# Newton's products of three normalizations kept in a PSUM bank, and y h y of one column as one operation

## The chip, the cores and the metric

The kernel runs on one core of a Trainium2 chip. The metric is the time of one execution on the device in microseconds (us); for the kernel before it is the median of three runs.

## What is computed

Two layers of a decoder trunk over 512 tokens of width 1024 in float32. Each layer is a half-step SwiGLU feed-forward (FFN a), a token mixer with three groups of heads (differential attention, dilated attention, RWKV-7), and a second half-step feed-forward (FFN b). A layer norm over the 1024 columns follows each of the three, and the RWKV-7 part normalizes its keys per head:

```python
def layer_norm(x, g, b):
    mu = jnp.mean(xf, -1, keepdims=True)
    var = jnp.mean(jnp.square(xf - mu), -1, keepdims=True)
    return (xf - mu) * lax.rsqrt(var + LN_EPS) * g + b
for l in range(DEPTH):
    x = layer_norm(ALPHA * x + 0.5 * swiglu(x, ffn_a...), ln_g[l, 0], ln_b[l, 0])
    ...                                    # input projection x @ w_in, three mixers
    kk = kk / jnp.maximum(jnp.sqrt(jnp.sum(jnp.square(kk), -1, keepdims=True)), 1e-12)
    ...
    x = layer_norm(ALPHA * x + mix @ w_out, ln_g[l, 1], ln_b[l, 1])
    x = layer_norm(ALPHA * x + 0.5 * swiglu(x, ffn_b...), ln_g[l, 2], ln_b[l, 2])
```

## The kernel before

**Tiling.** The 512 tokens are four tiles of 128 (t = 0 to 3). Every product runs as three float32r products of a high part and a low part (`mm3`, L85 to L87). A weight is split by ACT (`hi`, L79) and DVE (`lo`, L80) in the feed-forwards, and by ACT (`wh`) and POOL (`wl`, a subtraction of two SBUF tiles of 128x512) in the mixer.

**The reciprocal root.** `rsqrt_ops` (L89) starts from h = -v/2 (L94) and a first y by integer arithmetic (L97). Three Newton steps follow, of three DVE operations each: t = y y (L100), t = t h (L102), y = (t + 1.5) y (L104). All tiles are in SBUF, of n columns: n = 1 in the feed-forwards (one token tile), n = 2 in the norm behind the mixer (two token tiles at once), n = 8 in the keys, n = 4 and 8 in two other places (`rwkv_out`, `norms`).

**Feed-forward.** `project` (L145) makes the down projection. For each of the last token tiles `close` adds the accumulator, a PSUM bank, to x (L162), and takes statistics (L163); `norm_ops` (L129) then runs `bn_aggr` (L132), the Newton steps, and four operations on x of 128x512: x - mean times g (L139) and times the root plus b (L143). Tiles 0 and 1 come in the first half, their banks have the tag "r"; tiles 2 and 3 come last (tag "p1"), so that their norms stand between one stage and the next. A normalized tile is transposed on PE into PSUM banks (tag "m"), copied by ACT (`xhi`) and DVE (`xlo`). Here the framework's own scheduler orders the instructions.

**Mixer.** Streams (`keys`, `decays`, `columns`, `out`, `head` and others, in the order of `RANK`) are merged by `Board.merge`: it keeps an estimated time for every engine and tile, and counts free banks of each tag (`when`); the order that it emits is the order on each engine. A stream that needs a tag whose banks are all taken is held until another stream calls `drop`. In the trace all these operations have the line L504. At its start, columns for tokens 0 to 255 run on PE from tiles 0 and 1, and tiles 2 and 3 are transposed as soon as their norms of FFN a are done. `keys(j)` sums squares on PE into an "r" bank, copies them out (`ss`, a maximum with 1e-24), drops the bank, and runs the Newton steps with n = 8; PE then transposes the root. `out(half)` is the output projection of two tiles and their norm with n = 2; `head` begins FFN b on PE, with banks "p0" and "p1".

**Banks.** There are eight PSUM banks: two each of "p0", "p1", "m" and "r".

Of the kernel before, what the change touches and what calls it, by code (L numbers as in the profile page):

```python
# [8 lines left out]
FT = mybir.dt.float32  # L9
# [3 lines left out]
OP = mybir.AluOpType  # L13
# [4 lines left out]
NT = S // 128  # L18
# [9 lines left out]
class Trunk:  # L28
# [57 lines left out]
        mm(out, lh, rl, start=False, stop=False)  # L86
        mm(out, ll, rh, start=False, stop=last)  # L87

    def rsqrt_ops(self, pool, v, n, scale, eps, steps, vec):  # L89

        h = pool.tile([128, n], FT, name="rs_h", tag=f"rs_h{n}", bufs=2)
        y = pool.tile([128, n], FT, name="rs_y", tag=f"rs_y{n}", bufs=2)
        t = pool.tile([128, n], FT, name="rs_t", tag=f"rs_t{n}", bufs=2)
        vec.tensor_scalar(h, v, -0.5 * scale, -0.5 * eps, op0=OP.mult, op1=OP.add)  # L94
        yield y
        magic = 1597463007.0 - 2.0 ** 22 - 2.0 ** 30
        vec.tensor_scalar(y.bitcast(I32), h.bitcast(I32), -0.5, magic, op0=OP.mult, op1=OP.add)  # L97
        yield y
        for _ in range(steps):
            vec.tensor_tensor(t, y, y, op=OP.mult)  # L100
            yield y
            vec.tensor_tensor(t, t, h, op=OP.mult)  # L102
            yield y
            vec.scalar_tensor_tensor(y, t, 1.5, y, op0=OP.add, op1=OP.mult)  # L104
            yield y
# [20 lines left out]
    def stats(self, t):  # L126
        return self.const.tile([128, 2, 6], FT, name=f"st{t}", tag=f"st{t}", bufs=1)

    def norm_ops(self, ts, st, g, b, eps, vec):  # L129
        mv = self.const.tile([128, len(ts), 2], FT, name="mv", tag=f"mv{len(ts)}", bufs=2)  # L130
        for i, t in enumerate(ts):
            vec.bn_aggr(mv[:, i], st[t])  # L132
        for r in self.rsqrt_ops(self.const, mv[:, :, 1], len(ts), 1.0, eps, 3, vec):
            yield "."
        for i, t in enumerate(ts):
            x = self.x[t]
            for h in range(2):
                c = slice(h * 512, (h + 1) * 512)
                vec.scalar_tensor_tensor(x[:, c], x[:, c], mv[:, i, 0:1], g[:, 0, c], op0=OP.subtract, op1=OP.mult)  # L139
                yield "."  # L140
            for h in range(2):
                c = slice(h * 512, (h + 1) * 512)
                vec.scalar_tensor_tensor(x[:, c], x[:, c], r[:, i:i + 1], b[:, 0, c], op0=OP.mult, op1=OP.add)  # L143

    def project(self, h, w, alpha, eps, g, b, late):  # L145


        nc = self.nc
        nk = len(h)
        st = [self.stats(t) for t in range(NT)]  # L150

        def load(j, c):
            return self.weight(w[j * 256:(j + 1) * 256, c * 512:(c + 1) * 512].rearrange("(k p) c -> p k c", p=128), 2, 512)

        def step(acc, t, k, w2):
            hi, lo = h[k]
            s = slice(t * 128, (t + 1) * 128)
            self.mm3(acc, hi[:, s], lo[:, s], w2[0][:, k % 2, :], w2[1][:, k % 2, :], k == 0, k == nk - 1)

        def close(acc, t, c):  # L160
            xs = self.x[t][:, c * 512:(c + 1) * 512]
            nc.vector.scalar_tensor_tensor(xs, xs, alpha, acc, op0=OP.mult, op1=OP.add)  # L162
            nc.vector.bn_stats(st[t][:, c, :], xs)  # L163

        acc = [self.acc(("p0", "p1")[t // 2]) for t in range(NT)]
        for j in range(nk // 2):
            w2 = load(j, 0)
            for k in (2 * j, 2 * j + 1):
                for t in range(NT):
                    step(acc[t], t, k, w2)  # L170
        for t in range(NT):
            close(acc[t], t, 0)
        gt, bt = self.raw(self.row(g), 1, D), self.raw(self.row(b), 1, D)
        normed = []
        for half in range(2):
            ts = (2 * half, 2 * half + 1)
            acc = {t: self.acc("p1" if half else "r") for t in ts}
            tail = TAIL if half else 0
            for j in range(nk // 2 - tail):
                if half and j == TURN:  # L180
                    for t in normed:
                        self.to_channels(t)
                w2 = load(j, 1)
                for k in (2 * j, 2 * j + 1):
                    for t in ts:
                        step(acc[t], t, k, w2)
            rest = [(j, load(j, 1)) for j in range(nk // 2 - tail, nk // 2)]
            for t in ts:
                for j, w2 in rest:
                    for k in (2 * j, 2 * j + 1):  # L190
                        step(acc[t], t, k, w2)
                close(acc[t], t, 1)
                for _ in self.norm_ops((t,), st, gt, bt, eps, nc.vector):
                    pass
                if t not in late:
                    if half:
                        self.to_channels(t)
                    else:
                        normed.append(t)
# [163 lines left out]
class Board:  # L363
# [27 lines left out]
    def drop(self, *tiles):  # L391
        for t in tiles:
            r = self.ready[t.tensor.name]
            self.slots[r[3]].append(r[2])
            r[3] = "dropped"
# [118 lines left out]
class Mix:  # L514
# [360 lines left out]
    def keys(self, j):  # L875

        tr, P = self.tr, self.P
        vec, act, pe, sp = self.vec, self.act, self.pe, self.sp
        u, drop, ct = self.u, self.drop, self.ct
        v3 = lambda t, hf: t[:, hf * 256:(hf + 1) * 256].rearrange("p (c t) -> p c t", t=64)  # L880
        yield f"k{j}", "u"
        k = ct[f"k{j}"]
        q = u("kap")
        act.activation(q, k, AF.Square, scale=P("c_k_k", j))
        yield ".", "r"
        ps = self.acc("r", (128, NT, 2))
        for n in range(NT):
            pe.matmul(ps[:, n, :], q[:, n * 128:(n + 1) * 128], tr.pick, start=True, stop=True)
        yield "."
        ss = self.t("ss", (128, 8), bufs=2)  # L890
        vec.tensor_scalar(ss, ps.rearrange("p n e -> p (n e)"), 1e-24, None, op0=OP.max)
        drop(ps)
        for rs in tr.rsqrt_ops(self.pool, ss, 8, 1.0, 0.0, 3, vec):
            yield "."
        yield ".", "r"
        ps = self.acc("r", (2, S))
        for n in range(NT):
            pe.transpose(ps[:, n * 128:(n + 1) * 128], rs[:, 2 * n:2 * n + 2], tr.ident)
        act.copy(q[0:2], ps)
        drop(ps)  # L900
        yield ".", "r"
        ps = self.acc("r")
        pe.matmul(ps, self.c["sel"][0:2], q[0:2], start=True, stop=True)
        yield "."
        vec.scalar_tensor_tensor(q, k, P("c_k_k", j), ps, op0=OP.mult, op1=OP.mult)
        drop(ps)

        yield f"decays{j}", "u"
        a, dk, dr, db = self.key[j]
        t = u("kt")  # L910
        act.activation(t, a, AF.Identity, scale=P("c_k_a", j), bias=self.omka[:, j:j + 1])
        vec.tensor_tensor(a, a, q, op=OP.mult)
        yield "."
        vec.tensor_tensor(k, k, t, op=OP.mult)
        yield f"r{j}", ".", "u", "u"
        r = ct[f"r{j}"]
        vec.scalar_tensor_tensor(t, r, P("c_r_k", j), k, op0=OP.mult, op1=OP.mult)
        for hf in range(2):
            yield ".", "u"
            b = self.kr[j, hf] = u("kr", (128, 4, 2, 64))  # L920
            vec.tensor_tensor(b[:, :, 0, :], v3(q, hf), v3(dk, hf), op=OP.mult)
            vec.tensor_tensor(b[:, :, 1, :], v3(r, hf), v3(dr, hf), op=OP.mult)
            yield "."
            sp.dma_start(self.kd[j, hf], b.rearrange("p c e t -> p (c e t)"))
        drop(q, r, dk, dr)
        yield ".", "r"
        ps = self.acc("r", (128, NT, 2))
        for n in range(NT):
            pe.matmul(ps[:, n, :], t[:, n * 128:(n + 1) * 128], tr.pick, start=True, stop=True)
        act.copy(self.bon[:, :, 2 * j:2 * j + 2], ps)  # L930
        drop(ps, t)
        for hf in range(2):
            yield ".", "u"
            b = self.bk[j, hf] = u("bk", (128, 4, 2, 64))
            for e in range(2):
                p = HALF[e]
                vec.tensor_tensor(b[p, :, 1 - e, :], v3(a, hf)[p], v3(db, hf)[p], op=OP.mult)
                vec.tensor_tensor(b[p, :, e, :], v3(k, hf)[p], v3(db, hf)[p], op=OP.mult)
        drop(a, k, db)
        self.mark(f"keys{j}")  # L940
# [440 lines left out]
    def out(self, half):  # L1381
# [5 lines left out]
        for c in range(2):  # L1387
# [18 lines left out]
            for t in ts:  # L1406
# [6 lines left out]
                xs = tr.x[t][:, c * 512:(c + 1) * 512]  # L1413
                vec.scalar_tensor_tensor(xs, xs, ALPHA, acc[t], op0=OP.mult, op1=OP.add)
                vec.bn_stats(self.st[t][:, c, :], xs)
                self.drop(acc[t])
        yield from tr.norm_ops(ts, self.st, *self.gb, LN_EPS, vec)
        for t in ts:
            yield from tr.channel_ops(t, self.pe, self.act, vec, self.acc, self.drop)
            self.mark(f"new{t}")  # L1420
# [120 lines left out]
```

## Time and profile before

| | us |
|---|---|
| median of three runs | 2340.93 (2340.63 to 2344.64) |
| the profiled execution | 2363.04 |
| its span, first to last instruction | 2361.3 |
| PE busy | 2250.8 (95%) |
| DVE busy | 1153.8 (49%) |
| ACT busy | 804.7 (34%) |
| POOL busy | 317.3 (13%) |

The profile is of one execution, taken by the hardware profiler. A row of a timeline is: start, duration in us, engine, line, operation, output <- inputs by the program's names, and in brackets how long the engine sat idle before it and what it waited for. SBUF tiles and PSUM tiles are told apart by their names here: `p`, `m` and `r` are PSUM banks, all others lie in SBUF. PEclk is the granted TensorE clock as a share of its full speed.

### The profile page before, as it was taken

Reading aid. Unit: us, or ns where it says so; the run is one execution under the profiler, and the core shown is the slowest. Engines: PE = TensorE matmul, PEld = TensorE weight load, DVE = VectorE, ACT = ScalarE, POOL = GpSimd, SP = SyncE. Lnnn points to the kernel's source line nnn. Section 1 sums busy time; section 2 is a strip of 40 time slices with the busy share of each in tenths; the row PEclk is TensorE's granted clock in tenths of the full one; section 3 lists DMA queues with packets and bytes.
Section 4 is the critical chain, followed back from the end, with each engine's and each line's share of the span. In section 5 each row is a group of like instructions: output and inputs, shape, how many; then the busy total and the mean of one; then the engine's idle time right before and its main releaser. Section 6 shows DMA issues by size and latency. Waiting matters only on the chain.

```text
span 2361.3 us, 31781 instructions
## 1 busy us (share of the span) xinstructions
PE 2250.8 (95%) x12384; PEld 1878.7 (80%) x12384; DVE 1153.8 (49%) x2535; ACT 804.7 (34%) x1559; POOL 317.3 (13%) x344
## 2 busy tenths in 40 slices
PE   9999999987899999999999999999888998999998
PEld 8888888787777788888888888886877767888886
DVE  3333346666665633332653332567665667333336
ACT  4322233434444232222332222333454443222222
POOL 1000002343221300000010000023432222000000
PEclk9999999998887899999999999998998899999999
DMA  5333344354533223322543333443545333233334
GB/s 168 99 99 97 111 137 140 99 130 86 116 95 99 89 90 91 100 96 99 169 118 107 89 92 118 144 134 91 131 93 107 96 103 117 80 98 89 98 107 152
DMA packets 265702, 258.34 MB, mean 109 GB/s; under 512 B 56314, under 2 KB 213056, under 8 KB 265552
## 3 DMA queue, kind: packets, MB, share of 16 engines
q1 hardware_dynamic: 221488, 228.20, 32.0%
q0 software_dynamic: 43488, 27.06, 5.6%
q8 instruction: 97, 1.59, 0.3%
q10 hardware_dynamic: 576, 1.05, 0.1%
q14 instruction: 53, 0.43, 0.1%
HBM read 233.85 MB, written 22.28 MB: 108 GB/s over the span
## 4 chain that ended last, share of the span: by engine, by line
PE 81%; DVE 8%; DMA 5%; issue 3%; POOL 1%; ACT 1%; SPq 0%; POOLq 0%; DVEq 0%; ACTq 0%
PE p L86 18%; PE p L87 18%; PE p L85 18%; PE p L504 13%; PE r L504 4%; PE m L504 4%; DMA k<-qkA 3%; PE r L86 2%; PE r L85 2%; PE r L87 2%; DMA k<-qkB 1%; DVE x L504 1%; DVE rs_t L504 1%; POOL q L504 0%; POOL wl L504 0%
## 5 line engine op out<-in xcount | busy, mean ns | idle before, releaser
L80 DVE TENSOR_TENSOR lo<-raw,hi 128x1024 fp32r<-128x1024 f32 x300 | 366.2, 1223 | 634.9 <-ACT hi L79 634.3
L85 PE MATMUL p<-xhi,hi 128*128 128x512 f32 (+1 forms) x1392 | 538.0, 387 | 0.5 <-ACT xhi L118 0.5
L86 PE MATMUL p<-xlo,hi 128*128 128x512 f32 (+1 forms) x1392 | 537.7, 386 | 0.7 <-DVE xlo L119 0.7
L87 PE MATMUL p<-xhi,lo 128*128 128x512 f32 (+1 forms) x1392 | 537.5, 386 | 0.0
L79 ACT CAST hi<-raw 128x1024 fp32r<-128x1024 f32 x300 | 316.0, 1055 | 589.4 <-PE p L86 263.9
L86 PEld LDWEIGHTS p<-xlo,hi 128*128 128x128 f32 x1392 | 261.8, 188 | 58.8 <-DVE xlo L119 1.1
L85 PEld LDWEIGHTS p<-xhi,hi 128*128 128x128 f32 x1392 | 261.7, 188 | 58.8 <-ACT xhi L118 1.0
L87 PEld LDWEIGHTS p<-xhi,lo 128*128 128x128 f32 x1392 | 261.8, 188 | 57.9
L504 POOL TENSOR_TENSOR wl<-wr,wh 128x512 fp32r<-128x512 f32 x152 | 203.5, 1359 | 703.2 <-ACT wh L504 653.6
L504 PE MATMUL p<-wh,xhi 128*128 128x256 f32 (+1 forms) x704 | 236.1, 335 | 2.1 <-DVE rb L504 1.9
L504 PE MATMUL p<-wh,xlo 128*128 128x256 f32 (+1 forms) x704 | 219.9, 312 | 0.2 <-DVE xlo L504 0.2
L504 PE MATMUL p<-wl,xhi 128*128 128x256 f32 (+1 forms) x704 | 219.8, 312 | 0.0
L87 PE MATMUL p<-hi,hl 128*128 128x512 f32 x528 | 205.8, 390 | 0.0
L85 PE MATMUL p<-hi,hh 128*128 128x512 f32 x528 | 205.7, 390 | 0.0
L86 PE MATMUL p<-lo,hh 128*128 128x512 f32 x528 | 205.5, 389 | 0.0
L504 PEld LDWEIGHTS p<-wh,xhi 128*128 128x128 f32 x704 | 140.6, 200 | 13.3 <-PE p L504 2.3
L504 PEld LDWEIGHTS p<-wh,xlo 128*128 128x128 f32 x704 | 140.4, 199 | 7.0 <-DVE xlo L504 1.2
L239 DVE TENSOR_TENSOR hr<-p,hr 128x512 f32<-128x512 f32 x88 | 60.9, 692 | 172.8 <-PE p L87 163.3
L504 PEld LDWEIGHTS p<-wl,xhi 128*128 128x128 f32 x704 | 141.3, 201 | 4.3 <-POOL wl L504 0.3
L240 ACT CAST hh<-hr 128x512 fp32r<-128x512 f32 x88 | 54.3, 618 | 210.1 <-DVE hr L239 200.5
L504 ACT ACTIVATE t<-t,nm 128x128 f32<-128x128 f32 (+3 forms) x144 | 80.1, 557 | 128.0 <-DVE nm L504 127.0
L86 PEld LDWEIGHTS p<-lo,hh 128*128 128x128 f32 x528 | 99.1, 188 | 20.6
(247 smaller groups left out, 3104.3 us busy)
## 6 DMA issues: line engine op xcount, KB each, us to landing
raw<-in_ffn_a_down SPq DMA_DIRECT2D x66, 512.0 KB, 3.3
raw<-in_ffn_b_down SPq DMA_DIRECT2D x66, 512.0 KB, 3.4
raw<-in_ffn_a_gate SPq DMA_DIRECT2D x44, 512.0 KB, 3.8
raw<-in_ffn_a_up SPq DMA_DIRECT2D x44, 512.0 KB, 3.9
raw<-in_ffn_b_gate SPq DMA_DIRECT2D x40, 512.0 KB, 3.9
raw<-in_ffn_b_up SPq DMA_DIRECT2D x40, 512.0 KB, 3.8
wr<-in_w_in SPq DMA_DIRECT2D x56, 256.0 KB, 3.3
wr<-in_w_in SPq DMA_DIRECT2D x24, 512.0 KB, 3.8
```

Of the source, the lines that this page charges most:

```text
L79: nc.scalar.copy(hi, raw)
L80: (vec or nc.vector).tensor_tensor(lo, raw, hi.bitcast(FT), op=OP.subtract)
L85: mm(out, lh, rh, start=first, stop=False)
L86: mm(out, lh, rl, start=False, stop=False)
L87: mm(out, ll, rh, start=False, stop=last)
L239: nc.vector.tensor_tensor(hr, acc[1, f], hr, op=OP.mult)
L240: nc.scalar.copy(hi, hr)
L504: return call(*args, **kw)
```

## The change

`rsqrt_ops` takes a bank and writes t into its first columns instead of an SBUF tile; y and h stay in SBUF. With one column, t = y y and t = t h become one operation, t = (y h) y, with h as the scalar of each partition. `project` gives the accumulator's bank that `close` has just read; `out` gives the bank of the second tile's last accumulator and drops it when the whole norm is done; `keys` writes its sums and t into one bank, takes the maximum with 1e-24 inside the operation that makes h (so that the copy `ss` goes), and drops the bank when the root is done. `rwkv_out` and `norms` give no bank and stay as they were.

```diff
-    def rsqrt_ops(self, pool, v, n, scale, eps, steps, vec):
+    def rsqrt_ops(self, pool, v, n, scale, eps, steps, vec, bank=None, floor=None):
...
-        t = pool.tile([128, n], FT, name="rs_t", tag=f"rs_t{n}", bufs=2)
-        vec.tensor_scalar(h, v, -0.5 * scale, -0.5 * eps, op0=OP.mult, op1=OP.add)
+        t = pool.tile([128, n], FT, name="rs_t", tag=f"rs_t{n}", bufs=2) if bank is None else bank[:, 0:n]
+        if floor is None:
+            vec.tensor_scalar(h, v, -0.5 * scale, -0.5 * eps, op0=OP.mult, op1=OP.add)
+        else:
+            vec.tensor_scalar(h, v, floor, -0.5, op0=OP.max, op1=OP.mult)
...
         for _ in range(steps):
-            vec.tensor_tensor(t, y, y, op=OP.mult)
-            yield y
-            vec.tensor_tensor(t, t, h, op=OP.mult)
+            if n == 1:
+                vec.scalar_tensor_tensor(t, y, h, y, op0=OP.mult, op1=OP.mult)
+            else:
+                vec.tensor_tensor(t, y, y, op=OP.mult)
+                yield y
+                vec.tensor_tensor(t, t, h, op=OP.mult)
             yield y
             vec.scalar_tensor_tensor(y, t, 1.5, y, op0=OP.add, op1=OP.mult)
...
-                for _ in self.norm_ops((t,), st, gt, bt, eps, nc.vector):
+                for _ in self.norm_ops((t,), st, gt, bt, eps, nc.vector, acc[t]):
...
-        ps = self.acc("r", (128, NT, 2))
+        bank = self.acc("r", (128, 2, 8))
+        ps = bank[:, 0, :].rearrange("p (n e) -> p n e", e=2)
...
-        ss = self.t("ss", (128, 8), bufs=2)
-        vec.tensor_scalar(ss, ps.rearrange("p n e -> p (n e)"), 1e-24, None, op0=OP.max)
-        drop(ps)
-        for rs in tr.rsqrt_ops(self.pool, ss, 8, 1.0, 0.0, 3, vec):
+        for rs in tr.rsqrt_ops(self.pool, bank[:, 0, :], 8, 1.0, 0.0, 3, vec, bank[:, 1, :], 1e-24):
             yield "."
+        drop(bank)
...
-                self.drop(acc[t])
-        yield from tr.norm_ops(ts, self.st, *self.gb, LN_EPS, vec)
+                if not c or t == ts[0]:
+                    self.drop(acc[t])
+        bank = acc[ts[1]]
+        yield from tr.norm_ops(ts, self.st, *self.gb, LN_EPS, vec, bank)
+        self.drop(bank)
```

## Rows read from the trace of the kernel before

**Rows 1.** The page, part 4: shares of the chain that ended last, by engine.

```profile
PE 81%; DVE 8%; DMA 5%; issue 3%; POOL 1%; ACT 1%; SPq 0%; POOLq 0%; DVEq 0%; ACTq 0%
```

**Rows 2.** What PE waited for, whole span: us in total, times, longest.

```profile
PE m L504 <- DVE xlo L504: 13.9, 8, 3.6
PE r L504 <- DVE rs_y L504: 6.8, 4, 2.2
```

**Rows 3.** Timeline of DVE, layer 0, the end of FFN a, tiles 2 and 3.

```profile
382.37 0.15 DVE L100 TENSOR_TENSOR rs_t<-rs_y 128x1 f32<-128x1 f32 x1
382.56 0.16 DVE L102 TENSOR_TENSOR rs_t<-rs_t,rs_h 128x1 f32<-128x1 f32 x1
...
383.14 1.14 DVE L102 TENSOR_TENSOR rs_t<-rs_t,rs_h 128x1 f32<-128x1 f32 x1
...
387.24 2.41 DVE L143 SCALAR_TENSOR_TENSOR x<-x,rs_y,raw 128x512 f32<-128x512 f32 x2
389.58 0.67 DVE L162 SCALAR_TENSOR_TENSOR x<-x,p 128x512 f32<-128x512 f32 x1
```

**Rows 4.** Timeline of POOL in the same stretch.

```profile
382.97 2.54 POOL L504 TENSOR_TENSOR wl<-wr,wh 128x512 fp32r<-128x512 f32 x2 [1.33 <-ACT wh L504]
385.90 2.54 POOL L504 TENSOR_TENSOR wl<-wr,wh 128x512 fp32r<-128x512 f32 x2 [0.39 <-ACT wh L504]
```

**Rows 5.** Layer 0, output projection and norm of tiles 0 and 1: DVE, POOL.

```profile
791.90 0.69 DVE L504 SCALAR_TENSOR_TENSOR x<-x,p 128x512 f32<-128x512 f32 x1 [1.24 <-PE p L504]
...
801.07 1.13 DVE L504 TENSOR_TENSOR rs_t<-rs_y 128x2 f32<-128x2 f32 x1
...
791.28 1.29 POOL L504 TENSOR_TENSOR wl<-wr,wh 128x512 fp32r<-128x512 f32 x1 [7.38 <-ACT wh L504]
...
799.50 5.43 POOL L504 TENSOR_TENSOR wl<-wr,wh 128x512 fp32r<-128x512 f32 x4 [3.62 <-ACT wh L504]
```

**Rows 6.** Small DVE operations of three tiles: count, ns min/median/max, starts, forms.

```profile
L504 DVE SCALAR_TENSOR_TENSOR l<-l,nlam,r x48: 219/219/1331, 521.2 to 1816.7; 128x1 f32<-128x1 f32 x48
...
L504 DVE TENSOR_SCALAR ss<-r x4: 156/162/167, 418.7 to 1601.7; 128x8 f32<-128x8 f32 x4
...
L504 DVE TENSOR_SCALAR rs_h<-ssA x6: 156/158/161, 574.1 to 1854.3; 128x8 f32<-128x8 f32 x6
```

**Rows 7.** PE's stall behind it, layer 0, then stretches with PEclk (third from last).

```profile
396.52 1.97 PE L504 MATMUL m<-kept,x 128*128 128x128 f32 x8 [3.61 <-DVE xlo L504]
...
395.00:396.50 1.50, 0.00 (x0) 0.00 (x0) 1.50 (x4) 0.00 (x0) 0.00 (x0) 0.50 0.58 235
...
398.00:402.00 4.00, 4.00 (x22) 4.00 (x21) 1.38 (x2) 0.85 (x2) 0.00 (x0) 0.53 0.00 0
...
1573.50:1575.00 1.50, 1.50 (x9) 1.50 (x8) 1.07 (x2) 0.59 (x1) 0.00 (x0) 0.50 0.00 0
```

**Rows 8.** Layer 1, the end of FFN a: timelines of DVE and of POOL.

```profile
1557.73 0.15 DVE L100 TENSOR_TENSOR rs_t<-rs_y 128x1 f32<-128x1 f32 x1
...
1564.92 0.68 DVE L162 SCALAR_TENSOR_TENSOR x<-x,p 128x512 f32<-128x512 f32 x1
...
1558.38 5.16 POOL L504 TENSOR_TENSOR wl<-wr,wh 128x512 fp32r<-128x512 f32 x4 [1.39 <-ACT wh L504]
```

**Rows 9.** Timeline of PE, layer 0, around the first root of the keys.

```profile
423.70 0.95 PE L504 MATMUL r<-kept,kap 128*128 128x2 f32 x8
...
428.09 0.60 PE L504 MATMUL r<-kept,rs_y 128*2 128x128 f32 x4 [1.23 <-DVE rs_y L504]
```

**Rows 10.** Timeline of DVE at the end of the kernel, tile 3.

```profile
2351.94 0.68 DVE L162 SCALAR_TENSOR_TENSOR x<-x,p 128x512 f32<-128x512 f32 x1
...
2356.82 1.41 DVE L143 SCALAR_TENSOR_TENSOR x<-x,rs_y,raw 128x512 f32<-128x512 f32 x2
```

**Rows 11.** From FFN b of layer 0 to FFN a of layer 1: DVE, PE.

```profile
1196.83 0.16 DVE L104 SCALAR_TENSOR_TENSOR rs_y<-rs_t,rs_y 128x1 f32<-128x1 f32 x1
...
1196.60 1.04 PE L116 MATMUL m<-kept,x 128*128 128x128 f32 x8
```

More of the change, by code (lines that the diff above doesn't have):

```diff
@@ L127, in stats, with norm_ops @@
         return self.const.tile([128, 2, 6], FT, name=f"st{t}", tag=f"st{t}", bufs=1)
-    def norm_ops(self, ts, st, g, b, eps, vec):
+    def norm_ops(self, ts, st, g, b, eps, vec, bank):
         mv = self.const.tile([128, len(ts), 2], FT, name="mv", tag=f"mv{len(ts)}", bufs=2)
@@ L132, in norm_ops @@
             vec.bn_aggr(mv[:, i], st[t])
-        for r in self.rsqrt_ops(self.const, mv[:, :, 1], len(ts), 1.0, eps, 3, vec):
+        for r in self.rsqrt_ops(self.const, mv[:, :, 1], len(ts), 1.0, eps, 3, vec, bank):
             yield "."
```

## The prediction

> **What bounds the kernel now.** I read the chain that ended last, then PE's waits, then the timelines of DVE, POOL and PE where a changed norm stands on that chain. PE carries 81% of the chain and DVE 8% [rows 1], so an edit on DVE pays only where PE stands and waits for DVE. The waits name two such places in reach of the change: 13.9 us for `xlo`, the last step of a normalized tile, in 8 waits of up to 3.6, and 6.8 us for the root of the keys in 4 waits [rows 2]. In the middle of the feed-forwards PE does not wait for a norm, so tiles 0 and 1 there, and the four tiles of the first FFN b, I cost at nothing: PE's matmuls hide them. That cover has one weak spot, below.
>
> The reader is to see in [rows 3] that the same small operation on one column takes 0.16 us and, at 383.14, 1.14. Beside [rows 4], this one (and two more like it before 387.24) starts inside a POOL subtraction (1.27 us each, two in 2.54) and ends with it: 383.14 + 1.14 = 384.28, and POOL's first ends at 382.97 + 1.27 = 384.24. It has two SBUF inputs. An operation with one SBUF and one PSUM input does not stop: x at 791.90 took 0.69 us inside the POOL subtraction of 791.28 [rows 5]. So t in PSUM should free t h and (t + 1.5) y of this stop. It does not free y y, whose inputs are both y: at 801.07 it took 1.13 [rows 5]; nor y h y, which reads y twice.
>
> **Prices.** Two dependent small operations start 0.19 us apart (382.37, 382.56) [rows 3]. The fused one is, by form, a scalar_tensor_tensor of one column with a partition scalar: 219 ns [rows 6], 0.06 more than the 0.16 of the plain ones, so it takes 0.25 where two took 0.39. A step saves 0.14 and a root of one column 0.41 without any stop.
>
> PSUM as an operand of a small operation: read, it costs 162 ns (`ss`, from an "r" bank) against 158 (`rs_h` from SBUF) [rows 6]. Written by DVE it is shown nowhere. I bound it from -0.02 us (rather less than the scatter of the small rows) to +0.15, a whole small operation again, and take 0, because the read that is shown costs 4 ns. [...]
>
> **Part 1, FFN a into the mixer, twice.** DVE does the norm of tile 2, then of tile 3, then `xlo` of tile 2, and PE stands 3.61 us for that `xlo` [rows 7]. Layer 0, anew from 382.37: fused 0.25, y 0.19, fused at 382.81, y at 383.06, the third fused at 383.26. This lies in POOL's first subtraction and ends with it at 384.3; y until 384.5; the first half of L143, with two SBUF inputs, at 384.57 lies in the second (until 385.51) and ends at 386.2. POOL's third, due at 385.90, waits for it, runs from about 386.0, and holds the second half of L143 until 387.25 (in [rows 3] and [rows 4] the two engines take turns likewise); that ends at 387.95. Tile 3's L162 then starts at 387.9 instead of 389.58: 1.7 us. If DVE got two turns running it would be 2.7; if the third fused one also met the second subtraction, 0.7. Layer 1, with four subtractions from 1558.38 and Newton from 1557.73 [rows 8], comes out in the same way at 1563.2 instead of 1564.92: 1.7. Tile 3 meets no POOL work and saves 0.41. Together 2.1 a layer, and PE's stall is 1.5 instead of 3.6, so all of it reaches PE: **4.2 us** (2.2 to 6.2). POOL's own delay I cost at nothing: in [rows 4] it has stood idle for ACT before each pair, and nobody in that stretch waits for it.
>
> The clock comes with it. [...] In layer 1 at least 1.5 us was at half: 0.7 or more. A stall of 1.5 us ends before 395.0, where layer 0 shows half the clock; but the clock is not the change's to set. Bounds 0 and 3.4; I take **1.0**, nearer to nothing, since PE still stalls.
>
> **Part 2, the norm behind the mixer, twice.** Only tiles 0 and 1 meet POOL. Four subtractions cover 799.50 to 804.93 [rows 5], and DVE stops once in each of the last three. Now the stops move to y y, one in each step: the three remain. What is saved is what followed the last stop: four small operations, two afterwards, 0.4 us; behind it L143's twin meets POOL again and gives some back. **0.3 a layer, 0.6** (0 to 1.5). Tiles 2 and 3 meet no POOL and have the same number of operations: 0.
>
> **Part 3, the keys, four roots.** `ss` goes, 0.2 us on DVE. The first root of a layer is done long before its last step, which waits its turn in the order; for the second, `ss` stands between the operations that PE awaits at 428.09 [rows 9]. The planner counts one dependent operation less, so that a step of the first root may come one place earlier. **0.3 a layer, 0.6** (-1 to 2).
>
> **Part 4, the end, once.** Both last norms are in series on DVE: tile 3's L162 starts at 2351.94, when tile 2's is done, and the last operation is at 2356.82 [rows 10], with no POOL work. Two roots of 0.41: **0.8**.
>
> **Waits that are added.** The bank is released only after the root. In project, "p1" is taken next by FFN a's second layer and by the mixer's columns; in the former, tile 3's root ends at 1196.99 and PE wants that bank behind the transposes of 1196.60, at about 1197.5 [rows 11], so 0.5 us cover it, and the fused root ends earlier still: 0; if the cover went, PE would stand for the rest of the root, some tenths, once. In out, the last bank is dropped after the norm, and `head`'s fourth group of matmuls needs it: it is planned after the transposes of tile 2 instead of partly before them, the same work in another order: 0, with 0.6 a layer either way. In keys, see the third rival.
>
> **Sum.** 4.2 + 1.0 + 0.6 + 0.6 + 0.8 = 7.2 us. The profiled execution took 2363.04 us, 1.7 more than its span of 2361.3, where all of this was worked out; the median is 22.1 us (0.9%) below it, which changes 7.2 by less than 0.1. So 2340.9 - 7.2 = **2333.7 us**.
>
> **Rivals.**
> 1. PSUM is dear. At the middle of its bounds, 0.065 us for every operation that touches t, a root of one column gives back its 0.39 of 0.41: twice 0.78 in part 1, 0.4 in part 2 and 0.3 in part 3, and 0.8 at the end, 3.7 in all. 2337.4 us. The trace speaks against it with 162 to 158 ns for a read; for the write nothing speaks. [...]
> 2. The stall's gain is not carried. PE's chain through the mixer leans on DMA for 5% [rows 1] and on a fixed emitted order; if a transfer or another engine is late next, part 1 is given back there and parts 2 and 4 remain, 1.4 us: 2339.5. Against it: the chain in both layers runs through this very stall, and the transfers on it start from work behind the stall.
> 3. The other side: the "r" banks. Each key's sums used to leave their bank after `ss`; now the bank is kept until the root is done. From the second sums at 423.70 to the first root at 428.09 [rows 9] both banks are taken. No other user of "r" is ahead of PE there in the trace, and the planner won't emit one while both are taken; but a plan that shifts one by two tenths may put one of PE's products behind the bank, and all of PE's queue with it. Price: 4.3 us a layer, 8.6, and then half a clock behind it as after the 3.6 us stall, 3.4: 7.2 - 12.0, 4.8 slower, 2345.7. It decides from the point where one user of "r" comes between those two.
> 4. The change does not do what it says: the stops hold every DVE operation, not those with two SBUF inputs. Then the stops stay as many as they are, and only the fused operations and `ss` pay: tile 3 in part 1 (0.8), the keys (0.6) and the end (0.8), 2.2 together: 2338.7. The 0.69 at 791.90 speaks against it.
>
> **How the numbers follow.** Forecast 0.55, dear PSUM 0.16, not carried 0.10, "r" banks 0.10, no such effect 0.09. About 0.2% (4.7 us, below 2336.2 or above 2345.6) is what a measurement of this kernel can tell from no change. Of the forecast's own cases nine in ten are below 2336.2, and a third of the dear ones with the clock's gain: faster 0.55; slower 0.09, nearly all from the third rival; same 0.36. The range goes from the forecast with the clock's full 2.4 more and another 3 from DVE's second turns and the keys, 2328.3, up past the second rival, 2341.0.
>
> **What would show it.** Right: L104 and t h never at 1.1 us any more while y h y and y y still are; tile 3's L162 some 1.7 us nearer to tile 2's; PE's wait for `xlo` at 1.5 instead of 3.6 us in both layers; the fused operation near 219 ns and its successor 0.25 us later; the last norm 0.4 shorter. Wrong: small operations on the bank at 200 ns or more (rival 1); PE's stall shorter but the start of FFN b not earlier (rival 2); a new wait of PE in an "r" product between the keys' sums and the root (rival 3).

## The result, and the profile after

The changed kernel takes **2328.0 us** (median of six runs, 2316.6 to 2329.8) against 2341.6 before on the same chip. The ratio is 0.9928, 95% interval 0.9903 to 0.9953: 11 to 23 us faster. The forecast was 2333.7 us, in a range from 2328.3 to 2341.0. By the medians the gain is 13.6 us where 7.2 were forecast. The two profiles must not be subtracted from each other: with 2363 and 2317 us they lie 22 above and 11 below their medians.

The chain that ended last has the same shares [rows 1]:

```profile
PE 82%; DVE 8%; DMA 5%; issue 3%; POOL 1%; ACT 1%; SPq 0%; DVEq 0%; POOLq 0%; ACTq 0%
```

What PE waited for in the changed kernel, in total, times, longest [rows 2]:

```profile
PE m L511 <- DVE xlo L511: 11.3, 8, 2.4
...
PE r L511 <- DVE rs_y L511: 4.2, 2, 2.1
...
PE r L511 <- DVE rs_h L511: 3.0, 2, 1.5
```

The longest wait for `xlo` is 2.4 instead of 3.6 us. Below are DVE and POOL at the end of FFN a in layer 1, changed kernel [rows 3, 8]. Line numbers have moved: L105 is the fused operation, L111 the update of y, L146 the old L139, L150 the old L143, L169 the old L162.

```profile
1522.27 4.24 POOL L511 TENSOR_TENSOR wl<-wr,wh 128x512 fp32r<-128x512 f32 x3
1522.38 1.72 DVE L146 SCALAR_TENSOR_TENSOR x<-x,mv,raw 128x512 f32<-128x512 f32 x1
1524.03 1.25 DVE L105 SCALAR_TENSOR_TENSOR p<-rs_y,rs_h 128x1 f32<-128x1 f32 x1
1525.31 0.16 DVE L111 SCALAR_TENSOR_TENSOR rs_y<-p,rs_y 128x1 f32<-128x1 f32 x1
1525.51 1.03 DVE L105 SCALAR_TENSOR_TENSOR p<-rs_y,rs_h 128x1 f32<-128x1 f32 x1
1526.57 0.16 DVE L111 SCALAR_TENSOR_TENSOR rs_y<-p,rs_y 128x1 f32<-128x1 f32 x1
...
1528.55 0.68 DVE L169 SCALAR_TENSOR_TENSOR x<-x,p 128x512 f32<-128x512 f32 x1
```

Beside POOL's three subtractions the fused operation stops (1.25 and 1.03 us), and the update of y, which reads the bank, does not (0.16). Over the whole span, DVE operations on `p` banks by form, ns min/median/max:

```profile
L105 DVE SCALAR_TENSOR_TENSOR p<-rs_y,rs_h x24: 211/227/1252, 379.7 to 2310.5; 128x1 f32<-128x1 f32 x24
L111 DVE SCALAR_TENSOR_TENSOR rs_y<-p,rs_y x24: 134/157/158, 381.0 to 2310.7; 128x1 f32<-128x1 f32 x24
```

The end of the kernel, tile 3 [rows 10]: 4.49 us from the first row to the second, 4.88 before.

```profile
2306.45 0.68 DVE L169 SCALAR_TENSOR_TENSOR x<-x,p 128x512 f32<-128x512 f32 x1
...
2310.94 1.41 DVE L150 SCALAR_TENSOR_TENSOR x<-x,rs_y,raw 128x512 f32<-128x512 f32 x2
```

So far this is the mechanism of the forecast. What the forecast had not looked for stands in the stretches where PE is busy all the time and no changed operation is near.

### The profile page after: what moved, and what is told of

It reads as the page before. It is cut to its first block, busy times and chain, and to the rows that moved or that the text cites. A ratio compares the mean times of both kernels' runs of the same rounds, so it can differ in the third digit from the quotient of the medians.

```text
span 2315.4 us, 31736 instructions
## 1 busy us (share of the span) xinstructions
PE 2210.5 (95%) x12384; PEld 1861.4 (80%) x12384; DVE 1146.9 (50%) x2483; ACT 803.2 (35%) x1559; POOL 317.8 (14%) x344
## 4 chain that ended last, share of the span: by engine, by line
PE 82%; DVE 8%; DMA 5%; issue 3%; POOL 1%; ACT 1%; SPq 0%; DVEq 0%; POOLq 0%; ACTq 0%
PE p L86 18%; PE p L87 18%; PE p L85 18%; PE p L511 14%; PE r L511 4%; PE m L511 4%; DMA k<-qkA 3%; PE r L86 2%; PE r L87 2%; PE r L85 2%; DMA k<-qkB 1%; DVE x L511 1%; POOL wl L511 1%; DVE xlo L511 1%; DVE gy L511 0%
## 5 line engine op out<-in xcount | busy, mean ns | idle before, releaser
L85 PE MATMUL p<-xhi,hi 128*128 128x512 f32 (+1 forms) x1392 | 531.4, 382 | 0.5 <-ACT xhi L125 0.5
L87 PE MATMUL p<-xhi,lo 128*128 128x512 f32 (+1 forms) x1392 | 531.6, 382 | 0.0
L85 PEld LDWEIGHTS p<-hi,hh 128*128 128x128 f32 x528 | 99.1, 188 | 20.5
```

What stands on the lines that cost most here:

```text
L85: mm(out, lh, rh, start=first, stop=False)
```

## Experiments

Theory A: the norms in the feed-forwards carry the gain, with the clock behind PE's shorter stall. Theory B: the keys carry it, since the planner places their operations anew. Theory P came with the first results: not the operations carry it but the addresses in SBUF. All times are medians; differences in us are worked out from the ratio, against the kernel before on the same chip.

### Each part alone

The kernel before, unchanged:

> The kernel before, unchanged, for a second profile and for the scatter between equal kernels. The first profile took 2363 us against a median of 2341, and the profile of the changed kernel 2317 against 2328, so 45.9 us lie between them, of which only some 13 are the change. All theories: ratio 1.000 within 0.2%, about 2341 us. If the 1% by which PE's pitch in the feed-forwards differs between the two profiles belongs to the execution and not to the kernel, this profile shows another pitch than the first one, and single runs of it may lie near 2330 as well. If it belongs to the change, the pitch is that of the first profile again. The clock: if the half clock behind the norms of the first feed-forward a follows from PE's 3.6 us stall, it is there again, in both layers; if it was chance, it is missing in one or both.

Measured 0.999 (0.9966 to 1.0014), profile 2342 us. The half clock behind PE's stall was missing this time in both layers (mean granted clock of the whole execution 0.971, 0.959 in the first profile), and the stalls were 2.6 and 2.5 us; so part of what the first profile showed was chance.

The feed-forward norms alone (`norm_ops` gives the bank only in `project`, the fused operation as in the change):

> Only the feed-forward norms are changed (t in the accumulator's bank, y h y as one operation); the keys and the norm behind the mixer are as before. Theory A (the gain is that of the feed-forward norms with the clock behind them): 5 to 9 us faster, most of 13.6; tile 3's statistics come 0.7 to 1.7 us nearer to tile 2's, PE's wait for xlo falls from 3.6 to about 2 us, and the half clock behind it goes. Theory B (the gain is that of the keys, planned anew): 3 to 5 us faster, namely 0.7 + 1.7 from the two stalls, 2 x 0.4 at the tiles and the end, and at most 2 of clock. My forecast had 6.0 for these parts (4.2 + 1.0 + 0.8).

The keys alone (the diff's part in `keys`, nothing fused):

> Only the keys are changed: sums and t in one bank that is held until the root is done, and the maximum inside the operation that makes h, so that the copy goes. Theory A: 0.6 us faster (my forecast's term), within 0.2% of before. Theory B (the plan of the first roots moves): 5 to 8 us faster; the second root is done some 7 us nearer to the mixer's start in both layers (51 us behind it instead of 58), PE's two waits for the roots are 2.1 and 1.5 us instead of 3.4 and the attention starts earlier by 2 to 4 us a layer. The rival of the banks held: slower by up to 4.8, with a new wait of PE between the sums and the root.

The norm behind the mixer alone (the diff's part in `out`, nothing fused):

> Only the norm behind the mixer is changed: t of two columns in the bank of the second tile's last accumulator, which is dropped after the norm. Theories A and B: 0.6 us faster (0 to 1.5), not to be told from no change; y y still stops beside POOL's subtractions (1.1 us each), t h and y do not. Rival: the bank that is dropped later delays FFN b's start and makes it slower by some tenths to 2 us.

| | ratio | us |
|---|---|---|
| feed-forward norms alone | 0.9897 (0.9863 to 0.9932) | -24 |
| keys alone | 0.9992 (0.9968 to 1.0017) | -2 |
| mixer norm alone | 0.9913 (0.9886 to 0.9940) | -20 |
| whole change, the first measurement | 0.9928 (0.9903 to 0.9953) | -17 |

Neither A nor B can give this. Two parts together bring more than twice the whole, though each alone can't be told from the whole by its interval; and one of them is a norm of two tiles whose three stops on y y stayed. Where they gain shows in a window of the last feed-forward, 260 us in which PE is busy throughout at full clock. Columns: length, PE busy with its number of products, granted clock, DMA share, GB/s. The kernel before (again):

```profile
2000.00:2260.00 260.00, 260.00 (x1122) 1.00 0.32 96
```

The changed kernel:

```profile
2000.00:2260.00 260.00, 260.00 (x1141) 1.00 0.33 101
```

The same clock, the same busy time, and 1.7% more products. By form, products of the feed-forward, kernel before (again): line, operation, tiles, shape, count, busy us, mean ns of one:

```profile
L85 PE MATMUL p<-xhi,hi 128*128 128x512 f32 x1280 | 506.4, 396 | 0.0
L86 PE MATMUL p<-xlo,hi 128*128 128x512 f32 x1280 | 506.2, 396 | 0.0
...
L85 PE MATMUL p<-hi,hh 128*128 128x512 f32 x528 | 205.7, 390 | 0.0
```

The changed kernel:

```profile
L86 PE MATMUL p<-xlo,hi 128*128 128x512 f32 x1280 | 503.2, 393 | 0.0
...
L85 PE MATMUL p<-xhi,hi 128*128 128x512 f32 x1280 | 499.7, 390 | 0.0
...
L85 PE MATMUL p<-hi,hh 128*128 128x512 f32 x528 | 205.7, 390 | 0.0
```

The first products (x times gate and up weights) took 6 ns longer than equally large ones of the down projection, and lose 3 to 6 of them; the down projection stays. Products overlap, so that what counts in a busy stretch is the pitch, the time from the start of one to the start of the next. The first kind has 233.3 ns before, 228.9 after and 226.7 in the two runs that gained most; the second kind always has 227.

What the three faster kernels have in common is memory. `rs_t` of one column, `rs_t` of two columns and the keys' `ss` took 64 bytes per partition each (two buffers of 32). Where one is no longer allocated, all that is allocated behind it moves down. Addresses in the compiled programs, in bytes; in these products `xhi` is the moving operand and the weight the stationary one:

| kernel | weight ring `hi` | minus `xhi`, mod 256 | mixer weights `wh` | minus `xhi`, mod 256 |
|---|---|---|---|---|
| before | 96192 | 64 | 204736 | 64 |
| feed-forward norms alone, mixer norm alone | 96128 | 0 | 204672 | 0 |
| keys alone | 96192 | 64 | 204672 | 0 |
| changed kernel | 96064 | -64 | 204544 | -128 |

`xhi` lies at 16512 in all of them, `xlo` and `lo` 16384 behind `xhi` and `hi`. In the down projection both operands (`hh` and `hi`) move together, and their difference is 0 modulo 256 in every one of these kernels; its pitch is the 227 ns that never changed.

### Addresses alone, operations alone

The kernel before with one slot less, no operation changed:

```diff
-        h = pool.tile([128, n], FT, name="rs_h", tag=f"rs_h{n}", bufs=2)
+        ht = pool.tile([128, 2 * n if n == 1 else n], FT, name="rs_h", tag=f"rs_h{n}", bufs=2)
+        h = ht[:, 0:n]
...
+        t = ht[:, n:2 * n] if n == 1 else pool.tile([128, n], FT, name="rs_t", tag=f"rs_t{n}", bufs=2)
```

> The kernel before with every instruction as it was; only t of one column lies in the second half of h's slot, so that one SBUF slot of 64 bytes is not allocated and everything that is allocated behind it (the weight ring, the hidden tiles, the mixer's weights) lies 64 bytes lower. Theory P (the gain of the feed-forward run and of the mixer-norm run is where the weights lie): the products xhi, xlo by hi, lo of the feed-forwards start every 226.7 ns instead of 233.5, the mixer's 256-column products every 120 ns instead of 118, and the time is 18 to 26 us below that of before, with no norm changed at all. Theory A (the norms' operations bring the gain): no change, within 0.2%.

The changed kernel at the old addresses (the tile `rs_t` still allocated ahead of `t = bank[:, 0:n]`, `ss` too, neither used):

> The changed kernel with the SBUF tiles that it no longer needs (t of one and of two columns, the copy of the keys' sums) still allocated and unused, so that all weights lie where they lay before. Theory P: the feed-forward products start every 233.5 ns as before, and the time is 0 to 7 us below before (my forecast of 7.2 us for the operations alone belongs to this run). Theory A: all of the gain is still there, 13 us below before.

> The changed kernel as it is, for a comparison on the same chip. All theories: 11 to 23 us below before. Theory P: of that 16 to 18 us from the feed-forward's product pitch (229 ns at its addresses, 128 bytes lower than before), the rest, about nothing or a little lost, from operations and the mixer's pitch.

| | ratio | us |
|---|---|---|
| old operations, 64 bytes lower | 0.9902 (0.9870 to 0.9934) | -23 |
| new operations, old addresses | 0.9966 (0.9937 to 0.9995) | -8 |
| changed kernel | 0.9922 (0.9896 to 0.9948) | -18 |

The old norms gain 23 us by moving 64 bytes. In that kernel (the first of the table) the products of the gate and up weights are:

```profile
L85 PE MATMUL p<-xhi,hi 128*128 128x512 f32 x1280 | 498.2, 389 | 0.0
```

That is 8.2 us less than the 506.4 of before, in each of three such lines: 25 us. (The 4176 products of the expectations include 336 of 256 columns; these three lines are the 3840 of 512.) For the changed kernel the same sum is 6.7 + 3.0 + 6.0 = 15.7. All tiles of the kernel with the feed-forward norms alone lie where they lie in this one, and it gained 24: at these addresses, too, the operations can't be told apart by the time.

### The pitch by itself

Behind the last norm, when no other engine works, 30 bursts of 24 products with `xhi` as the moving and a scratch tile as the stationary operand, in one execution:

> The kernel before with some 780 extra products behind its last norm, when no other engine works: bursts of 24 products of 512 columns (and some of 256) whose stationary operand is shifted by 0 to 960 bytes against the position of xhi, the moving one, and bursts in which the moving one is shifted or both are. The bursts' names give the shifts in bytes. Theory P in its simplest form (what counts is the position of the stationary operand relative to the moving one): bursts with equal shifts of both take 227 ns a product whatever the shift, those with the stationary one 64 bytes further 231 to 236, those 192 further (64 behind) 226 to 232. If the position of one of them alone counts, the bursts in which both are shifted differ from the one with none. If it takes work of other engines, all bursts show the same pitch. The time of the whole kernel is some 180 us longer.

Means of one by form (s: shift of the stationary, m: of the moving operand, in bytes; w: 512 columns, h: 256):

```profile
L1506 PE MATMUL s0w<-xhi,w 128*128 128x512 f32 x24 | 5.6, 389 | 0.0
L1506 PE MATMUL s64w<-xhi,w 128*128 128x512 f32 x24 | 5.8, 396 | 0.0
L1506 PE MATMUL s128w<-xhi,w 128*128 128x512 f32 x24 | 5.8, 395 | 0.0
L1506 PE MATMUL s192w<-xhi,w 128*128 128x512 f32 x24 | 5.7, 392 | 0.0
L1506 PE MATMUL s256w<-xhi,w 128*128 128x512 f32 x24 | 5.6, 389 | 0.0
L1506 PE MATMUL s64m64w<-xhi,w 128*128 128x512 f32 x24 | 5.6, 391 | 0.0
L1506 PE MATMUL s0h<-xhi,w 128*128 128x256 f32 x24 | 3.0, 282 | 0.0
L1506 PE MATMUL s192h<-xhi,w 128*128 128x256 f32 x24 | 3.0, 279 | 0.0
```

Pitches of 512 columns, by the shift of the stationary operand: 226.7 ns at 0 and 256 bytes, 233.4 at 64 and 320, 229.3 at 192, 448, 704 and 960, 233.1 to 233.9 at 32, 96, 128, 160 and 224 (232.3 at 384, 640 and 896). With the moving operand shifted by 64 instead, 229.3, as with the stationary one at 192. With both shifted by the same 64, 128 or 192 bytes, the bursts begin at 224 to 236 and settle at 227. So what counts is the position of one operand relative to the other, modulo 256 bytes, and no other engine is needed for it. With 256 columns it is the other way round and smaller: 120 ns settled at 0, 117.8 at 64 and 192, which is what the mixer shows (120 ns in the kernels at 0, 118 before).

### Which operations, at the same addresses

With the unused slots still allocated, so that the weights lie as before:

> Only the feed-forward norms are changed, and the unused slots stay allocated, so that all weights lie where they lay. By my forecast's terms 4.2 + 1.0 + 0.8 = 6.0 us below before. By the profiles so far: 1.6 us a layer from PE's shorter stall, about 0.9 a layer from the clock behind it and 0.75 at the end, 5.8 together. If the forecast's stops do not exist, only the fused operations pay: 0.8 + 0.8. Tile 3's statistics come 8.65 us behind tile 2's (9.3 to 10.5 in the kernels with the old norm).

> Only the keys are changed, and the unused slots stay allocated, so that the mixer's weights lie where they lay (in the earlier run of the keys alone they had moved 64 bytes, where 256-column products take 120 ns instead of 118). Theory B, of the plan: some 2.5 us a layer, 5 us below before; the six products of columns that stood behind the second root come ahead of it. My forecast: 0.6 us. If the earlier null result holds at the same place too: no change.

The fused operation without a bank (nothing passes `bank`):

> The feed-forward norms with y h y as one operation but with t in SBUF; no bank anywhere, keys and mixer norm as before, all weights where they lay. By the forecast's rule (an operation with two SBUF inputs stops beside POOL's subtraction) the y update can still stop: tile 3's statistics 9.3 to 10.5 us behind tile 2's as before, less 0.4, so 0.4 to 0.8 a layer and 0.75 at the end: 1.5 to 2.5 us below before. If the bank does not matter and one operation less is what counts: tile 3 at 8.65 and 5 to 6 us below before, as with the bank.

The bank without the fused operation (`if n == 0:` in place of `if n == 1:`, slots kept):

> Only the feed-forward norms are changed, with t in the bank but y y and t h as two operations; the unused slots stay allocated, so that all weights lie where they lay. By the forecast's rule y y can stop beside POOL's subtraction and the other two cannot: of three operations a step one stops, as with the fused one; tile 3's statistics come 8.6 to 9.1 us behind tile 2's (0.4 more than with both), the end is not shorter, and the time is 1 to 5 us below before. If the fused operation is what counts, tile 3 is at 9.3 to 10.5 as before.

| at the old addresses | ratio | us | tile 3's statistics behind tile 2's, layers 0, 1 |
|---|---|---|---|
| feed-forward norms | 0.9981 (0.9958 to 1.0004) | -4.5 | 8.64, 8.64 |
| keys | 1.0007 (0.9987 to 1.0026) | +1.6 | 10.41, 10.41 |
| fused, no bank | 0.9989 (0.9970 to 1.0008) | -2.6 | 9.94, 9.93 |
| bank, not fused | 0.9979 (0.9948 to 1.0010) | -4.9 | 7.42, 8.46 |

By the time none of the four is clear of no change. Theory B falls: the keys bring nothing that can be measured. Their operations did move, but PE's waits for the roots are 4.2 + 3.0 us in that run against 6.8 [rows 2].

The last column shows what the bank does. In the kernel with the fused operation and no bank, layer 1, DVE stands beside two of POOL's subtractions, from 1534.61 on (2.84 us together):

```profile
1534.97 1.24 DVE L105 SCALAR_TENSOR_TENSOR rs_t<-rs_y,rs_h 128x1 f32<-128x1 f32 x1
1536.25 1.22 DVE L111 SCALAR_TENSOR_TENSOR rs_y<-rs_t,rs_y 128x1 f32<-128x1 f32 x1
1537.50 0.22 DVE L105 SCALAR_TENSOR_TENSOR rs_t<-rs_y,rs_h 128x1 f32<-128x1 f32 x1
```

The changed kernel at the old addresses, same place, with subtractions from 1543.61 on (2.77 us, two):

```profile
1543.91 1.25 DVE L107 SCALAR_TENSOR_TENSOR p<-rs_y,rs_h 128x1 f32<-128x1 f32 x1
1545.20 0.16 DVE L113 SCALAR_TENSOR_TENSOR rs_y<-p,rs_y 128x1 f32<-128x1 f32 x1
1545.39 1.01 DVE L107 SCALAR_TENSOR_TENSOR p<-rs_y,rs_h 128x1 f32<-128x1 f32 x1
```

The same operation, y from t, in the second subtraction: 1.22 us with t in SBUF, 0.16 with t in PSUM. But the stop that y escapes is met by the next fused operation, 1.01 us. Over both norms the bank wins one stop: without it four DVE operations between the two tiles' statistics take over 0.9 us, with it three.

### Closing the account

The old operations with x and all weights at the changed kernel's addresses (`t` of one and two columns in h's slot, `ss` in the slots of `rs_t8`; some small tiles and vectors of the mixer lie 64 bytes elsewhere), beside the changed kernel:

> The kernel before with every operation as it was, but with the addresses of the changed kernel: t of one and of two columns lies in the second half of h's slot and the copy of the keys' sums shares the slots of another small tile, so that the weight ring lies 128 bytes lower and the mixer's weights 192. Theory P: products at 229.3 ns in the feed-forwards (4176 x 4.2 = 17.5 us less) and about 119 instead of 118 in the mixer (some 2100 to 3000 products, 2 to 3 us more): 15 us below before, and 2 to 8 us above the changed kernel. If the operations carry the gain of the changed kernel: no change against before.

> The changed kernel beside the old operations at its addresses, on the same chip. Theory P: 16 to 20 us below before, 2 to 8 below the old operations at the same addresses. If the operations carry the gain: 13 to 20 below those too.

0.9914 (0.9884 to 0.9944) against 0.9924 (0.9891 to 0.9956): 20 and 18 us below before. At these addresses the operations cannot be told apart by the time. In the profile of this run of the changed kernel one feed-forward (layer 0, b) ran at the longer pitch, though the addresses are the same. Its products from 845 to 1110 us are:

```profile
L85 PE MATMUL p<-xhi,hi 128*128 128x512 f32 x287 | 114.0, 397 | 0.0
```

In the first profile of the changed kernel they are:

```profile
L85 PE MATMUL p<-xhi,hi 128*128 128x512 f32 x278 | 109.0, 392 | 0.0
```

The pitch is 233.3 ns instead of 228.9, which costs some 4 us. At 0 and at 64 the feed-forwards of all profiles had one pitch each, 226.7 and 233.3; at -64 there are two, in one feed-forward of 16.

The scatter between executions comes from elsewhere. The mixers, from tile 2's last statistics in FFN a to the first statistics of the norm behind the mixer, differ with the granted clock. The kernel before, then the changed kernel, first profiles, layers 0 and 1, columns as above:

```profile
380.67:799.41 418.74, 377.88 (x2720) 0.87 0.39 102
1556.03:1965.91 409.88, 366.33 (x2728) 0.92 0.41 103
377.05:774.35 397.30, 357.95 (x2720) 0.94 0.41 107
1521.34:1924.43 403.09, 363.45 (x2728) 0.93 0.41 105
```

| stretches | before | changed kernel |
|---|---|---|
| the feed-forwards | 1434.3 | 1417.6 |
| the two mixers | 828.6 | 800.4 |
| the rest | 98.4 | 97.4 |
| span | 2361.3 | 2315.4 |

The feed-forwards' stretches begin at the start, or with FFN b's first product behind `head`, and end with tile 2's last statistics ahead of a mixer or of the end. Of the 46 us between these two profiles 28 are the mixers' and 17 the feed-forwards'. In all profiles but the probe's the mixers take 798 to 829 us. The feed-forwards follow the addresses: 1432 to 1435 us with the ring at 64, 1418 at -64 (1423 with the one at 233.3 ns), 1408 to 1412 at 0, with old operations and with new. So the addresses are worth 16 us to the changed kernel, about what it gained.

### A better place

The changed kernel with one unused slot of 64 bytes (`rs_t` of one column still allocated): the ring at 0, the mixer's weights at -64.

> The changed kernel with one unused SBUF slot of 64 bytes, so that the weight ring lies 64 bytes lower than before (a multiple of 256 from xhi) and the mixer's weights 128 bytes lower (a multiple of 256, less 64). Theory P, with the pitches of the probe: feed-forward products every 226.7 ns instead of 233.5, so 4176 x 6.8 ns = 28 us less; the mixer's 256-column products at 117.8 as before; and the operations' 8 us: some 33 us below before, 25 to 40, and faster than the changed kernel and than every run so far. If position is not what counts, it is as the changed kernel, 13 to 20 us below before.

> The best place with the change as it is, again, for the comparison on one chip: 24 to 27 us below before (25.7 in its first run), 28 to 35 if the pitches add up with the operations' 3 to 8 us.

The same place, with the bank and two operations where POOL works, fused only in the last feed-forward:

> The kernel of the best place (weight ring 64 bytes lower than before, mixer's weights 128), with t in the bank in all feed-forward norms, but y y and t h as two operations, except in the last feed-forward, where no POOL works and y h y stays one operation. If fewer and shorter stops of DVE beside POOL reach the end: PE's stall before the third tile's transposes 1.5 to 1.8 us instead of 2.06 in both layers, and 0 to 1 us faster than the best place with the change as it is, not to be told from it by the time. If the shorter stall of the bank without the fused operation was only POOL's chance position in that run: stalls of 2.0 to 2.5 us.

0.9897 (0.9873 to 0.9922) and 0.9895 (0.9871 to 0.9919), 2318.8 and 2318.4 us: 24 us below before. It is the fastest of the kernels with the whole change, some 10 us below the changed kernel by the medians, though the intervals overlap. The 33 us expected were not reached: by the rows the pitches bring 25 and not 28, and the operations less than the 8 us that were added (below). The mixed kernel, 0.9900 (0.9869 to 0.9931), adds nothing: PE's stalls were 1.4 and 3.05 us, so the short stalls of the bank without the fused operation were POOL's position in that run.

## Why the prediction was wrong

**The step that failed** is the sentence "an edit on DVE pays only where PE stands and waits for DVE", and with it the middle of the feed-forwards, costed at nothing because PE does not wait for a norm there. The diff also stops allocating three small tiles, and by that moves the weights against `xhi`. In those stretches, where PE never waits, its products then take 15.7 us less by their rows, and the mixer's some 2 us more (by the bursts 118.7 ns instead of 117.8 for each of 2496 products of 256 columns): some 13 in all. The old operations with the weights at the new addresses measure that with 20 (13 to 27), and the feed-forwards' stretches with 16. No rival of the prediction stood against this. A sign was there: products of 512 columns took 396 ns in one stage and 390 in the next, both with PE busy throughout, and I read only waits.

**Part 1** (4.2 us): the kind of gain was right, the size too large, and its parts came out otherwise. For tile 2 the forecast's 1.7 us came: tile 3's statistics are 8.65 us behind tile 2's in 15 of the 16 boundaries with the change (9.70 in layer 0 of its first profile), 10.34 in both layers of the profile I worked from [rows 3, 8]. But the three operations that stop are not the three of the forecast. POOL's subtractions now start 0.9 us behind tile 2's statistics and not 2.2 to 2.7, and the second half of L146 (1.72), the first fused operation and the second one stop (rows of the result); both halves of L150 run free. That this comes to 1.7 us as well is luck. For tile 3 the forecast had 0.41 less, because it "meets no POOL work". Now it does, in the same 15 boundaries, and takes 0.16 us more from its statistics to `xlo` (4.93 against 4.77). Layer 1 of the changed kernel, POOL, DVE and PE's stall behind them:

```profile
1528.00 3.03 POOL L511 TENSOR_TENSOR wl<-wr,wh 128x512 fp32r<-128x512 f32 x2 [1.49 <-ACT wh L511]
1530.30 1.28 DVE L146 SCALAR_TENSOR_TENSOR x<-x,mv,raw 128x512 f32<-128x512 f32 x1
1535.64 1.26 PE L511 MATMUL m<-kept,x 128*128 128x128 f32 x8 [1.92 <-DVE xlo L511]
```

So PE's stall is 2.0 us and not the 1.5 of the forecast. And in four of the 14 boundaries with the old norm (the probe's left aside) tile 3 was at 9.3 already, according to where POOL stands; PE's stall was 3.3 us on the mean of the 14 (2.4 to 3.7). That makes 1.3 a layer, 2.6 in all. I had carried one execution's phase of two engines through to a tenth.

**The clock** (1.0): no run shows this term, an estimate from one execution as is its bound of 3.4; what the runs showed in its place is that around that stall PE's granted clock was at half (0.50) for 3.4 us on the mean of the old norm's 14 boundaries, in 3.0 of which PE worked, and for 1.5 on the mean of the new one's 16. That is 0.75 us of work a layer, 1.5 in all. Right in kind, and two thirds of the size; it varies from 0 to 6.8 us with the old norm and from 0 to 3.4 with the new.

**Part 2** (0.6): of the wrong sign, mostly. It had said that L143's twin, the operations on x behind the root, "meets POOL again and gives some back", and counted 0.3 a layer as left. From the norm's statistics to `xlo` it takes 13.5 to 13.8 us in all 22 boundaries with the old norm behind the mixer. With the new one it takes 13.3 in 3 of 16, which is the forecast's 0.3, and 14.2 to 14.3 in the other 13. There the operations on x stop three times and not twice, and PE's stall behind them is 3.9 us where it was 0.8 to 1.8. (One operation of the norm that has one SBUF input, `rs_h`, takes 1.06 us beside the first subtraction, before and after; the forecast's rule of two inputs does not cover it.) Layer 0 before, and the changed kernel in its run beside the old operations:

```profile
806.98 3.42 DVE L504 SCALAR_TENSOR_TENSOR x<-x,rs_y,gb 128x512 f32<-128x512 f32 x2
810.33 1.40 DVE L504 SCALAR_TENSOR_TENSOR x<-x,mv,gb 128x512 f32<-128x512 f32 x2
811.65 1.40 DVE L504 SCALAR_TENSOR_TENSOR x<-x,rs_y,gb 128x512 f32<-128x512 f32 x2
813.71 1.97 PE L504 MATMUL m<-kept,x 128*128 128x128 f32 x8 [1.54 <-DVE xlo L504]
...
785.45 2.42 DVE L511 SCALAR_TENSOR_TENSOR x<-x,rs_y,gb 128x512 f32<-128x512 f32 x2
787.79 2.42 DVE L511 SCALAR_TENSOR_TENSOR x<-x,mv,gb 128x512 f32<-128x512 f32 x2
790.14 2.45 DVE L511 SCALAR_TENSOR_TENSOR x<-x,rs_y,gb 128x512 f32<-128x512 f32 x2
793.25 1.97 PE L511 MATMUL m<-kept,x 128*128 128x128 f32 x8 [3.90 <-DVE xlo L511]
```

On the mean 0.5 us a layer is lost, 1.0 in all, and about 0.7 a layer more to the clock behind the longer stall (PE worked 3.7 us at half the clock there, 2.3 with the old norm). The kernel with this norm alone shows the 3.9 us in both layers, so it belongs to this part; why POOL's third subtraction comes earlier was not tried.

**Part 3** (0.6): no gain by the time (1.6 us slower, between 6.1 slower and 3.0 faster). By the rows PE worked 7.4 us at half the clock (0.50) around the second root on the mean of 18 boundaries with the new keys and 9.4 on that of 20 with the old, 1.0 us of work a layer; the times can't confirm that.

**Part 4** (0.8): right; from tile 2's last statistics to the end it is 14.10 us in all profiles of the old norm and 13.35 of the new.

**Added waits** (0): right for the keys and `project`; what PE waits for the roots is 4.2 + 3.0 us after and 6.8 before [rows 2], under two names now. The third rival, the banks held, did not happen.

**Prices.** The fused operation takes 227 ns (219 estimated). PSUM as an output costs little: y y of the keys' eight columns takes 174 ns (median) in the bank, 161 for all such operations in SBUF before. The first rival falls: y reads the bank in 157 ns, and took 159 from SBUF.

The operations together, by the rows: 2.6 + 1.5 + 0.75 for the feed-forward norms, 1.0 + 1.4 lost behind the mixer's norm, 2.0 won and 0.4 lost at the keys, some 4 us. By the time they are worth 8 us (1 to 15) at the old addresses, 4.5 (10 faster to 1 slower) without keys and mixer norm, and nothing at the new addresses (2331.4 and 2331.3 us by the medians). My 7.2 lies within the first interval, but the times don't settle it, and by the rows it was too much. The total came out larger by the term that was missing.

## What to carry to other kernels

A change that frees or adds a tile moves every tile behind it; compare the addresses of the two programs first, and separate the two effects by keeping the old slot allocated and unused. When equal products show different times from start to start in stages where the engine never waits, ask where their operands lie: here the moving and the stationary operand of 512-column products want the same position modulo 256 bytes (226.7 ns a product, 229.3 to 233.9 at the other shifts), and 64 bytes of placement are worth more than three rewritten norms (23 us against 8). Compare profiles stretch by stretch: here the mixers, whose time follows the granted clock (418.7 us at 0.87, 397.3 at 0.94), hid what the feed-forwards showed. A stall that hangs on the phase of two engines should be priced from several executions, not from one row; taking one stop away can hand it to the next operation (1.01 us here), or make a longer one elsewhere (PE's 3.9 us behind the mixer's norm).

## What the runs showed of the hardware

Float32r products of 512 columns start, in the probe, every 226.7 ns when both operands lie alike modulo 256 bytes, 233.4 when the stationary one is 64 further, 229.3 (in the kernel 228.9, and once 233.3) when it is 64 behind; of 256 columns every 120, 117.8 and 117.8. The cause inside the engine was not tried.

DVE operations of one column with two SBUF inputs took 1.0 to 1.3 us beside POOL's subtractions and 0.15 to 0.23 otherwise (medians); with one of the two in PSUM they took 0.16 beside them (the changed kernel, at its own and at the old addresses).
